# Activations split in one go, dependent sums spread over turns, and an eleventh chunk as seven block products

## The chip, the cores and the metric

The kernel runs on one core of one Trainium2 chip. The metric is the device time of one execution in microseconds. Five engines work side by side, each in the order of its own instruction stream: PE (matrix products; PEld is its weight load), DVE (elementwise, also on sums), ACT (elementwise with a function), POOL, and SP, which here only issues transfers. They wait for each other through semaphores.

## The reference, cut to what matters

One layer of a hybrid decoder trunk on 256 rows of 1024 features, all in float32. The change lies in its last part, the MLP, where D_FF is 4096:

```python
n = RMSNorm(x)
h = x + W_mix_out(g_conv * ConformerConv(n) + g_attn * DSA(n))
h = h + CrossAttn(RMSNorm(h), RMSNorm(mem))
hf = _rmsnorm(h, norm_ffn_g[l]) @ w_ff1[l]
h = h + jnp.square(jax.nn.relu(hf)) @ w_ff2[l]
return _rmsnorm(h, norm_final_g)
```

## The kernel before

**Numbers.** A float32 operand is kept as two parts, a high one (ACT copies it into a rounded type) and a low one (DVE subtracts the high one from the operand). A product is three matmuls, high by high, high by low and low by high (`mm3`, L348). So every weight costs ACT and DVE one pass each before PE can use it.

**The MLP stage.** It is the last stage, from about 325 us on. The 4096 hidden features are cut into 16 chunks of 256. Chunk c has a first weight f1(c), 1024 by 256, cut into two sides of 128 columns, and a second weight f2(c), 256 by 1024. The loop at L1304 takes c from 0 to 12 and works two chunks ahead on the first product. For a chunk in `SEVEN` an iteration has six turns, in this order on PE: `first(c+2, side 0)`, the f2(c) pieces `left` and `last`, `first(c+2, side 1)`, and the pieces `outer` and `inner`. `first` is 24 matmuls of 256 columns; the four pieces are 6, 3, 6 and 6 matmuls of 512 columns. What follows chunk 12 is written out by hand from L1316 on.

**Seven or eight block products.** Hidden chunk times f2(c) is a 2 by 2 block product for each of the two row blocks. A chunk not in `SEVEN` does it as eight block products of 512 columns (24 matmuls). A chunk in `SEVEN` (L60) does it as seven (21 matmuls), in the manner of Strassen: some of the factors are sums of blocks. The sums of f2 are made by DVE (`seven`, L214: `outer` makes two sums in one instruction, `inner` two more, each needing the one before), the differences of the hidden blocks by DVE too (`fn`, L1179). Sums and their split copies live in the pool `t8`.

**Weights.** `load` (L164) issues the next 1 MB weight from HBM on SP's queue into one of three buffers `raw`, so it waits until the weight three places earlier has been read to the end. f1 and f2 alternate in the stream, so f2(c+1) goes into the buffer of f1(c+2). `high_jobs` is a queue of splitting jobs in the order in which PE wants the pieces. Every turn calls `split_ahead` (L314): `split_low` (L280) lets DVE make the low part of the job of the turn before, and then runs the sums of the second job in the queue, if it has any; `split_high` (L273) takes the first job and lets ACT make its high part. The load of a later weight is called from the low part of a weight's last piece (L269, L246).

**Chains.** What follows a first product is a generator (`activation`, L1164), moved on by one step at every `tick` (L318), one tick per turn: ACT applies relu and squares, DVE makes the differences, ACT makes the high part `fs`, DVE the low part. Before, side 0 and side 1 are squared and split each on its own, and for a chunk in `SEVEN` side 1 has three differences in one step. `x.done()` (L1309) runs chains by further ticks until chunk c's are at their end.

**PSUM.** A first product goes to a bank of the tag `mm` (L143), which has two. From chunk 2 on the block product `7` holds one of them to the end of the loop (L1228), so all first products share the other: PE may start `first(c+2, side 1)` only after ACT has read side 0 out of it (the relu at L1166).

Of the kernel before, what the change touches and what calls it, by code (L numbers as in the profile page):

```python
# [8 lines left out]
F32 = mybir.dt.float32  # L9
# [7 lines left out]
P = 128  # L17
# [39 lines left out]
HALVES = 6  # L57
EARLY = (3,)
WHOLE = (("conv", 0),)
SEVEN = (2, 3, 4, 6, 7, 8, 9, 10, 11, 12)  # L60
JOINED = 13
BY_HALVES = tuple(("f1", i) for i in (4, 5, 6, 7))

# [51 lines left out]
def block_kernel(ctx, tc, x, xt, mem, memt, wst, wki, vecs, convw, gout, out):  # L115
# [21 lines left out]
    def w2(name, dt=F32, shape=(P, 512)):  # L137
        return work.tile(list(shape), dt, tag="w2", bufs=8, name=name)

    def bank(tag, bufs, name):  # L140
        return psum.tile([P, 512], F32, tag=tag, bufs=bufs, name=name)

# [58 lines left out]

    class Stage:

        def __init__(self, key, high, before=None, slot=True):
            self.key, self.high, self.before, self.slot = key, high, before, slot
            if not slot:
                elsewhere.add(key)

        def prepare(self):
            if self.before:  # L210
                self.before()
                self.before = None

    def seven(key, c, raw):  # L214

        b = raw.rearrange("p (k h n) -> p k h n", k=2, h=2)
        flat = raw.rearrange("p (j n) -> p j n", j=4)
        sums = []

        def outer():  # L220
            sums.append(t8(f"sums{c}", F32, (P, 4, 512)))
            dve.tensor_tensor(out=sums[0][:, 0:2, :], in0=flat[:, 0:4:3, :],
                              in1=flat[:, 1:2, :].to_broadcast([P, 2, 512]), op=ALU.add)

        def inner():
            t = sums[0]
            dve.tensor_tensor(out=t[:, 2, :], in0=t[:, 1, :], in1=flat[:, 0, :], op=ALU.add)
            dve.tensor_tensor(out=t[:, 3, :], in0=t[:, 2, :], in1=flat[:, 2, :], op=ALU.add)

        def stage(name, src_of, n, before=None):  # L230
            def high():
                src = src_of()
                if before:
                    both = t8(f"{name}{c}", F32R, (P, 2, 2, 512))
                    hi, lo = both[:, 0], both[:, 1]
                else:
                    hi = highs.tile([P, N_CHUNK // 2], F32R, tag="hi", name=f"hi{c}{name}")
                    lo = lows.tile([P, N_CHUNK // 2], F32R, tag="lo", name=f"lo{c}{name}")
                    hi, lo = (w[:, : n * 512].rearrange("p (j n) -> p j n", j=n) for w in (hi, lo))
                act(hi, src, AF.Copy)  # L240
# [9 lines left out]
            return Stage((*key, name), high, before, not before)  # L250

        return [stage("left", lambda: b[:, :, 0, :], 2), stage("last", lambda: flat[:, 3:4, :], 1),
                stage("outer", lambda: sums[0][:, 0:2, :], 2, outer), stage("inner", lambda: sums[0][:, 2:4, :], 2, inner)]

    def high(key, c, raw, ns, q, last):
        n = ns.stop - ns.start
# [16 lines left out]
    def split_high():  # L273
        if high_jobs and (not high_jobs[0].slot or nsplit[0] - nused[0] < HALVES - held[0]):
            job = high_jobs.pop(0)
            nsplit[0] += job.slot
            job.prepare()
            job.high()

    def split_low():  # L280
        if low_jobs:
            low_jobs.pop(0)()
        if len(high_jobs) > 1:
            high_jobs[1].prepare()

    nsplit, nused, held = [0], [0], [1]

# [149 lines left out]
    load()  # L437
    zero = w2("zero")
    nc.vector.memset(zero, 0.0)
    zero_r = cst.tile([P, 512], F32R, name="zero_r")  # L440
    nc.vector.tensor_copy(zero_r, zero)
    ident = cst.tile([P, P], F32, name="ident")
    make_identity(nc, ident)
# [6 lines left out]
    ki2 = cst.tile([P, S], F32, name="ki2")  # L450

    nc.scalar.activation(half, half, AF.Sigmoid, bias=0.0, scale=0.0)
    nc.gpsimd.memset(half, -0.5)
# [185 lines left out]
    tick()  # L639
    wi = cst.tile([P, 2, 8], F32, name="wi")  # L640

    bias = [cst.tile([P, P * (qb + 1)], F32, name=f"bias{qb}") for qb in range(2)]

    def causal(t, qb, value):
        tail = t[:, qb * P :]
# [19 lines left out]
    def index_scores():  # L665
# [3 lines left out]
        dve.tensor_copy(wi, ps[:, :16].rearrange("p (r h) -> p r h", r=2))  # L669
        for qb in range(2):  # L670
            nk = P * (qb + 1)
            score = cst.tile([P, nk], F32, name=f"score{qb}")
# [488 lines left out]
    start(turn_rows())  # L1161
    start(ff_scale())

    def activation(c, ct, ps, t, sh, sl):  # L1164
        if ps.shape[1] == S:
            act(t[:, ct, :], ps, AF.Relu)  # L1166
        else:
            yield from merge(t[:, ct, :], ps)
            yield
            act(t[:, ct, :], t[:, ct, :], AF.Relu)  # L1170
        act(t[:, ct, :], t[:, ct, :], AF.Square)
        yield
        flat = t.rearrange("p k (r n) -> p (k r) n", r=2)
        if c not in SEVEN:
            cs = [(slice(2 * ct, 2 * ct + 2), flat[:, 2 * ct : 2 * ct + 2, :])]
        else:
            cs = [(slice(1, 3), flat[:, 2:4, :]) if ct else (slice(0, 1), flat[:, 0:1, :])]
        if ct and c < JOINED:
            n = w2(f"fn{c}", F32, (P, 4, P))  # L1179
            if c in SEVEN:  # L1180
                dve.tensor_tensor(out=n[:, 0:2, :], in0=flat[:, 1:2, :].to_broadcast([P, 2, P]), in1=flat[:, 0:4:3, :],
                                  op=ALU.subtract)
                dve.tensor_tensor(out=n[:, 2, :], in0=flat[:, 0, :], in1=n[:, 1, :], op=ALU.subtract)
                dve.tensor_tensor(out=n[:, 3, :], in0=flat[:, 2, :], in1=n[:, 2, :], op=ALU.subtract)
                cs.append((slice(3, 7), n))
            else:
                dve.tensor_tensor(out=n[:, 0:2, :], in0=flat[:, 0:4:2, :], in1=flat[:, 1:4:2, :], op=ALU.subtract)
                cs.append((slice(4, 6), n[:, 0:2, :]))
        for js, src in cs:
            act(sh[:, js, :], src, AF.Copy)  # L1190
        yield
        for js, src in cs:
            dve.tensor_tensor(out=sl[:, js, :], in0=src, in1=sh[:, js, :].bitcast(F32), op=ALU.subtract)

    class Hidden:

        def __init__(self, c):
            self.c, self.jobs = c, []
            parts = t8(f"fs{c}", F32R, (P, 2, 7, P))
            self.hi, self.lo = parts[:, 0], parts[:, 1]  # L1200
            self.t = w2(f"ft{c}", F32, (P, 2, S))

        def after(self, ct, ps):
            self.jobs.append(start(activation(self.c, ct % 2, ps, self.t, self.hi, self.lo)))
# [2 lines left out]
            return self.hi[:, j, :], self.lo[:, j, :]  # L1207

        def row(self, k, rb):
            return self.of(2 * k + rb)  # L1210

        def done(self):
            for job in self.jobs:
# [31 lines left out]
            seventh(x, name)  # L1245
            tick()

    TERMS = {"left": (("1", 0), ("2", 1)), "last": (("3", 6),), "outer": (("5", 4), ("7", 3)), "inner": (("6", 5), ("4", 2))}

    def seventh(x, name):  # L1250
        w = weights("f2", x.c, name, None)
# [18 lines left out]
        return ap.rearrange("p (k f) -> p k f", f=P)  # L1270

    def last_residual(rb, ps, lo, hi):
        h = h_rm[:, lo // P : hi // P, rb, :]
        ps = by_tiles(ps)
        dve.scalar_tensor_tensor(out=h, in0=ps, scalar=r2[0][:, rb : rb + 1], in1=h, op0=ALU.mult, op1=ALU.add)

    def last_squares(rb, n, lo, hi):

        h = h_rm[:, lo // P : hi // P, rb, :]
        junk = w2(f"junk_o{rb}{n}")  # L1280
        act(by_tiles(junk[:, : hi - lo]), h, AF.Square, scale=1.0 / 32, accum_out=ss[:, rb, n : n + 1])
        if hi == D:
            dve.scalar_tensor_tensor(out=ss[:, rb, 0:1], in0=ss[:, rb, 0:1], scalar=EPS,
                                     in1=ss[:, rb, 1:2] if n == 2 else zero_c, op0=ALU.add, op1=ALU.add)
        dve.tensor_tensor(out=by_tiles(hg[:, rb, lo:hi]), in0=h, in1=by_tiles(g_out[lo // 512][:, lo % 512 : lo % 512 + hi - lo]), op=ALU.mult)

    def last_norm(rb, n):
        ms = small.tile([P, 1], F32, tag="mso", name=f"ms_o{rb}")
        dve.tensor_tensor(out=ms, in0=ss[:, rb, 0:1], in1=ss[:, rb, n : n + 1], op=ALU.add)
        nc.gpsimd.tensor_tensor(out=rs[:, rb : rb + 1], in0=ms, in1=half[:, 0:1], op=ALU.pow)  # L1290
        scale = rs[:, rb : rb + 1]
        for n, (lo, hi) in enumerate(((0, 352), (352, 704), (704, D))):
            cols = hg[:, rb, lo:hi]
            if n < 2:
                dve.tensor_scalar(cols, cols, scale, None, ALU.mult)
            else:
                act(cols, cols, AF.Copy, scale=scale)
            (nc.scalar if n == 2 else nc.sync).dma_start(out[rb, :, lo:hi], cols)

    def add_to(rb, hf, ps, scales):  # L1300
        h = h_rm[:, 4 * hf : 4 * hf + 4, rb, :]
        dve.scalar_tensor_tensor(out=h, in0=by_tiles(ps), scalar=scales[:, rb : rb + 1], in1=h, op0=ALU.mult, op1=ALU.add)

    for c in range(JOINED):  # L1304
        hidden.append(Hidden(c + 2))
        x, later = hidden[c], hidden[c + 2]
        wide = c not in SEVEN and c != 5
        first(later, 0, wide)
        x.done()  # L1309
        if c in (0, 1, JOINED - 1):  # L1310
            split_ahead()
        half_of(x, 0)
# [130 lines left out]
```

## Time and profile before

| | us |
|---|---|
| runs | 505.32, 505.08, 504.98; median 505.08 |
| profiled execution, its own time | 505.25 |
| its span, first to last instruction | 503.5 |
| mean granted TensorE clock | 0.998 |
| ACT busy over the span | 349.1 |
| DVE busy from 394.76 to 458.55 us (63.79 us) | 62.01 |
| PE busy in the same stretch | 63.66 |

The span is 1.75 us shorter than the execution's time; that difference lies ahead of the first and behind the last instruction. Durations below come from this one execution. An instruction's duration holds a tail in which the next one on the engine may already run, so what an engine spends on a row of instructions is read from their starts. Views used are the page, the chain of work that ended last, the waits, and the timeline, whose rows give start, duration, engine, line, operation, output<-inputs and in brackets the idle time ahead of it. `lo` and `hi` are parts of a weight; `hi70left` belongs to the weight with number 70 in the stream, and f2(c) has number 54+2c.

### The profile page before, as it was taken

How to read it: one execution, taken by the hardware profiler on the slowest of the kernel's cores; microseconds unless marked ns; L12 is line 12 of the kernel's file. 1: busy time of each engine (PE TensorE's matmuls, PEld its weight loads, DVE VectorE, ACT ScalarE, POOL GpSimd, SP SyncE). 2: the span in 40 equal slices, each digit the busy share in tenths (PEclk: the TensorE clock that was granted, in tenths of full speed). 3: DMA queues.
4: the chain of work that ended last, by engine and by line, in shares of the span. 5: the costliest groups of instructions: out<-in, count | busy, mean ns of one | idle time of the engine just before them, and what ended most of it. 6: DMA issues, size and time to landing. Idle time of an engine off the chain costs nothing.

```text
span 503.5 us, 8292 instructions
## 1 busy us (share of the span) xinstructions
PE 493.6 (98%) x3119; PEld 444.1 (88%) x3119; DVE 459.9 (91%) x858; ACT 349.1 (69%) x639; POOL 31.6 (6%) x49
## 2 busy tenths in 40 slices
PE   7999999999999999999999999999999999999995
PEld 5999998888888888888889999988989899988984
DVE  5999999999999799999988986888999899999994
ACT  7657777788656676668756667586777677777832
POOL 2002212221021100000000000000000000000000
PEclk9999999999999999999999999999999999999999
DMA  8949678899787744345645454368855645544602
GB/s 312 381 184 280 185 191 261 226 246 262 225 265 215 191 148 144 119 158 197 246 169 218 175 174 161 127 192 214 239 181 184 235 159 206 221 178 168 251 1 84
DMA packets 27225, 100.36 MB, mean 199 GB/s; under 512 B 10656, under 2 KB 11552, under 8 KB 17200
## 3 DMA queue, kind: packets, MB, share of 16 engines
q1 hardware_dynamic: 23120, 92.90, 53.4%
q0 software_dynamic: 3632, 6.59, 7.3%
q8 instruction: 24, 0.39, 0.3%
q10 hardware_dynamic: 432, 0.33, 0.2%
q14 instruction: 17, 0.14, 0.1%
HBM read 91.16 MB, written 1.05 MB: 183 GB/s over the span
## 4 chain that ended last, share of the span: by engine, by line
PE 62%; DVE 18%; ACT 7%; DMA 7%; issue 5%; POOLq 0%; POOL 0%; DVEq 0%; ACTq 0%
PE ps_conv L80 10%; DMA raw<-in_wst_dram 6%; PE ps_f L80 6%; DVE lo L80 5%; PE ps_ao L80 4%; PE ps_q L80 4%; PE ps_k L80 4%; PE ps_ga L80 4%; PE ps_gc L80 4%; PE ps_v L80 4%; PE ps_xo L80 3%; DVE sums L80 3%; PE ps_qi L80 2%; PE ps_xk L80 2%; PE ps_p L80 2%
## 5 line engine op out<-in xcount | busy, mean ns | idle before, releaser
L80 DVE TENSOR_TENSOR lo<-raw,hi 128x1024 fp32r<-128x1024 f32 x141 | 170.5, 1214 | 5.2 <-ACT hi L263 5.1
L263 ACT ACTIVATE hi<-raw 128x1024 fp32r<-128x1024 f32 x141 | 146.7, 1046 | 2.0 <-DMA raw<-in_wst_dram 2.0
L80 PE MATMUL ps_f<-ff_p,hi 128*128 128x256 f32 (+1 forms) x448 | 92.8, 299 | 0.6 <-ACT ft L1166 0.3
L80 DVE SCALAR_TENSOR_TENSOR acc<-u,cw,acc 128x234 f32<-128x234 f32 (+29 forms) x190 | 78.0, 461 | 0.3
L80 PEld LDWEIGHTS ps_f<-ff_p,hi 128*128 128x128 f32 x448 | 72.8, 191 | 5.8 <-ACT ft L1166 2.0
L80 PE MATMUL ps_f<-ff_p,lo 128*128 128x256 f32 x256 | 70.9, 282 | 0.0
L80 PEld LDWEIGHTS ps_f<-ff_p,lo 128*128 128x128 f32 x256 | 48.8, 191 | 0.6
L80 PE MATMUL ps_conv<-n_p,hi 128*128 128x256 f32 x224 | 41.0, 285 | 0.0
L80 PEld LDWEIGHTS ps_conv<-n_p,hi 128*128 128x128 f32 x224 | 34.9, 192 | 0.8 <-issue 0.7
L80 PE MATMUL ps_conv<-n_p,lo 128*128 128x256 f32 x112 | 31.7, 283 | 0.0
L588 POOL DMA_DIRECT2D acc<-products x25 | 21.6, 864 | 125.1 <-ACT products L587 50.1
L80 PE MATMUL ps_p<-hi,fs 128*128 128x512 f32 (+1 forms) x88 | 27.2, 372 | 0.0
L80 PE MATMUL ps_q<-n_p,hi 128*128 128x512 f32 x64 | 23.6, 406 | 0.0
L80 PE MATMUL ps_k<-n_p,hi 128*128 128x512 f32 x64 | 23.5, 407 | 0.0
L80 PE MATMUL ps_ao<-o_p,hi 128*128 128x512 f32 x64 | 22.6, 401 | 0.0
L80 PE MATMUL ps_co<-u_p,hi 128*128 128x512 f32 (+1 forms) x80 | 22.2, 351 | 0.0
L80 PE MATMUL ps_mix<-mix_p,hi 128*128 128x512 f32 (+1 forms) x80 | 22.2, 351 | 0.0
L80 PE MATMUL ps_ga<-n_p,hi 128*128 128x512 f32 x64 | 22.0, 396 | 0.0
L80 PE MATMUL ps_gc<-n_p,hi 128*128 128x512 f32 x64 | 22.0, 396 | 0.0
L587 ACT ACTIVATE products<-u,cw 128x231 f32<-128x231 f32 (+24 forms) x50 | 21.9, 489 | 0.0
L80 PEld LDWEIGHTS ps_conv<-n_p,lo 128*128 128x128 f32 x112 | 21.5, 192 | 0.0
L80 PE MATMUL ps_v<-hi,n_p 128*128 128x512 f32 x64 | 19.9, 389 | 0.0
(386 smaller groups left out, 1215.8 us busy)
## 6 DMA issues: line engine op xcount, KB each, us to landing
raw<-in_wst_dram SPq DMA_DIRECT2D x76, 1024.0 KB, 4.9
acc<-products POOLq DMA_DIRECT2D x25, 256.0 KB, 5.3
raw<-in_wst_dram SPq DMA_DIRECT2D x12, 512.0 KB, 7.6
x_rm<-in_x_dram SPq DMA_DIRECT2D x2, 512.0 KB, 4.2
mem_rm<-in_mem_dram SPq DMA_DIRECT2D x1, 1024.0 KB, 8.9
mem_t<-in_memt_dram SPq DMA_DIRECT2D x1, 1024.0 KB, 10.9
h_t<-in_xt_dram SPq DMA_DIRECT2D x1, 1024.0 KB, 7.0
h_rm<-turned SPq DMA_DIRECT2D x16, 64.0 KB, 5.6
```

Of the source, the lines that this page charges most:

```text
L80: return fn(*args, **kwargs)
L263: act(hi, raw[:, ns], AF.Copy)
L587: act(prod[:, a, s:], u[:, t, : S - s], AF.Copy, scale=cw[:, t, TAPS - 1 - s : TAPS - s])
L588: nc.gpsimd.dma_start(acc[:, ts, :], prod, accum_op=ALU.add)
```

## The change

Three things change in the MLP stage; tiles are also packed differently.

- `SEVEN` gets chunk 5, so chunks 2 to 12 are all done as seven block products.
- The sums of f2 become steps. `split_low` runs one step of the first of the next three jobs that has any, and not all sums of the second job at once. `inner` is two steps.
- The activation waits for both sides: side 0 only gets its relu, then both are squared in one instruction, the differences are made in three separate steps, and high and low parts are one instruction each over seven blocks (six or four for the other chunks). The last chunk, 15, keeps a split by sides. Row blocks are taken in swapped order so that the seven blocks lie side by side; `h_rm` and the output rows are indexed to match.
- `x.done()` goes ahead of `first(later, 0, wide)`.
- `ft` has a pool tag of its own with two buffers; `zero_r`, `ki2`, `bias` and `score` share that space before the MLP.

```diff
-SEVEN = (2, 3, 4, 6, 7, 8, 9, 10, 11, 12)
+SEVEN = (2, 3, 4, 5, 6, 7, 8, 9, 10, 11, 12)
...
+    def w4(name, dt=F32, shape=(P, KT, P)):
+        return work.tile(list(shape), dt, tag="w4", bufs=2, name=name)
...
-        def inner():
+        def inner(j):
             t = sums[0]
-            dve.tensor_tensor(out=t[:, 2, :], in0=t[:, 1, :], in1=flat[:, 0, :], op=ALU.add)
-            dve.tensor_tensor(out=t[:, 3, :], in0=t[:, 2, :], in1=flat[:, 2, :], op=ALU.add)
+            dve.tensor_tensor(out=t[:, j, :], in0=t[:, j - 1, :], in1=flat[:, 2 * j - 4, :], op=ALU.add)
...
-                stage("outer", lambda: sums[0][:, 0:2, :], 2, outer), stage("inner", lambda: sums[0][:, 2:4, :], 2, inner)]
+                stage("outer", lambda: sums[0][:, 0:2, :], 2, (outer,)),
+                stage("inner", lambda: sums[0][:, 2:4, :], 2, (lambda: inner(2), lambda: inner(3)))]
...
             nsplit[0] += job.slot
-            job.prepare()
+            while job.steps:
+                job.step()
             job.high()
 
     def split_low():
         if low_jobs:
             low_jobs.pop(0)()
-        if len(high_jobs) > 1:
-            high_jobs[1].prepare()
+        for job in high_jobs[:3]:
+            if job.steps:
+                job.step()
+                break
...
+    def part(c, t, js, sh, sl):
+        act(sh[:, js, :], t, AF.Copy)
+        yield
+        dve.tensor_tensor(out=sl[:, js, :], in0=t, in1=sh[:, js, :].bitcast(F32), op=ALU.subtract)
...
     def activation(c, ct, ps, t, sh, sl):
...
+        yield from relu(ps, t[:, 2 * ct : 2 * ct + 2, :].rearrange("p r n -> p (r n)"))
+        if ct == 0:
+            return
+        act(t[:, 0:4, :], t[:, 0:4, :], AF.Square)
+        yield
+        js = slice(0, 4)
+        if c in SEVEN:
+
+            dve.tensor_tensor(out=t[:, 4:6, :], in0=t[:, 0:1, :].to_broadcast([P, 2, P]), in1=t[:, 1:3, :], op=ALU.subtract)
             yield
+            dve.tensor_tensor(out=t[:, 6, :], in0=t[:, 1, :], in1=t[:, 5, :], op=ALU.subtract)
+            yield
+            dve.tensor_tensor(out=t[:, 7, :], in0=t[:, 3, :], in1=t[:, 6, :], op=ALU.subtract)
+            yield
+            js = slice(1, 8)
...
+        yield from part(c, t[:, js, :], slice(0, js.stop - js.start), sh, sl)
...
         wide = c not in SEVEN and c != 5
+        x.done()
         first(later, 0, wide)
-        x.done()
```

More of the change, by code (lines that the diff above doesn't have):

```diff
@@ L202, in block_kernel, with __init__, step @@
     class Stage:
-        def __init__(self, key, high, before=None, slot=True):
-            self.key, self.high, self.before, self.slot = key, high, before, slot
+        def __init__(self, key, high, steps=(), slot=True):
+            self.key, self.high, self.steps, self.slot = key, high, list(steps), slot
             if not slot:
                 elsewhere.add(key)
[L209 to L212, printed above, removed]
+        def step(self):
+            self.steps.pop(0)()
     def seven(key, c, raw):
@@ L223, in outer, with stage @@
                               in1=flat[:, 1:2, :].to_broadcast([P, 2, 512]), op=ALU.add)
-        def inner():
+        def inner(j):
             t = sums[0]
-            dve.tensor_tensor(out=t[:, 2, :], in0=t[:, 1, :], in1=flat[:, 0, :], op=ALU.add)
-            dve.tensor_tensor(out=t[:, 3, :], in0=t[:, 2, :], in1=flat[:, 2, :], op=ALU.add)
-        def stage(name, src_of, n, before=None):
+            dve.tensor_tensor(out=t[:, j, :], in0=t[:, j - 1, :], in1=flat[:, 2 * j - 4, :], op=ALU.add)
+        def stage(name, src_of, n, steps=()):
             def high():
                 src = src_of()
-                if before:
+                if steps:
                     both = t8(f"{name}{c}", F32R, (P, 2, 2, 512))
@@ L248, in high @@
                 low_jobs.append(low)
-            return Stage((*key, name), high, before, not before)
+            return Stage((*key, name), high, steps, not steps)
         return [stage("left", lambda: b[:, :, 0, :], 2), stage("last", lambda: flat[:, 3:4, :], 1),
-                stage("outer", lambda: sums[0][:, 0:2, :], 2, outer), stage("inner", lambda: sums[0][:, 2:4, :], 2, inner)]
+                stage("outer", lambda: sums[0][:, 0:2, :], 2, (outer,)),
+                stage("inner", lambda: sums[0][:, 2:4, :], 2, (lambda: inner(2), lambda: inner(3)))]
     def high(key, c, raw, ns, q, last):
@@ L439, in block_kernel @@
     nc.vector.memset(zero, 0.0)
-    zero_r = cst.tile([P, 512], F32R, name="zero_r")
+    zero_r = w4("zero_r", F32R, (P, 512))
     nc.vector.tensor_copy(zero_r, zero)
@@ L449, in block_kernel @@
     nc.gpsimd.memset(table, 0.0)
-    ki2 = cst.tile([P, S], F32, name="ki2")
+    picked = w4("picked", F32, (P, D))
+    ki2 = picked[:, 3 * S :]
     nc.scalar.activation(half, half, AF.Sigmoid, bias=0.0, scale=0.0)
@@ L640, in block_kernel @@
     wi = cst.tile([P, 2, 8], F32, name="wi")
-    bias = [cst.tile([P, P * (qb + 1)], F32, name=f"bias{qb}") for qb in range(2)]
+    bias = [picked[:, :P], picked[:, P : 3 * P]]
     def causal(t, qb, value):
@@ L671, in index_scores @@
             nk = P * (qb + 1)
-            score = cst.tile([P, nk], F32, name=f"score{qb}")
+            score = picked[:, (3 + qb) * P : (3 + qb) * P + nk]
             per = 512 // nk
@@ L1162, in block_kernel @@
     start(ff_scale())
-    def activation(c, ct, ps, t, sh, sl):
[L1165 to L1168, printed above, removed]
-            yield
[L1170 to L1193, printed above, removed]
@@ new lines, in relu, with by_halves @@
+    def relu(ps, t):
+        if ps.shape[1] == S:
+            act(t, ps, AF.Relu)
+        else:
+            yield from merge(t, ps)
+            yield
+            act(t, t, AF.Relu)
+    def part(c, t, js, sh, sl):
+        act(sh[:, js, :], t, AF.Copy)
+        yield
+        dve.tensor_tensor(out=sl[:, js, :], in0=t, in1=sh[:, js, :].bitcast(F32), op=ALU.subtract)
+    def by_halves(c, ct, ps, t, sh, sl):
+        js = slice(2 * ct, 2 * ct + 2)
+        yield from relu(ps, t[:, js, :].rearrange("p r n -> p (r n)"))
+        act(t[:, js, :], t[:, js, :], AF.Square)
+        yield
+        yield from part(c, t[:, js, :], js, sh, sl)
@@ new lines, in activation @@
+    def activation(c, ct, ps, t, sh, sl):
+        if c == 15:
+            yield from by_halves(c, ct, ps, t, sh, sl)
+            return
+        yield from relu(ps, t[:, 2 * ct : 2 * ct + 2, :].rearrange("p r n -> p (r n)"))
+        if ct == 0:
+            return
+        act(t[:, 0:4, :], t[:, 0:4, :], AF.Square)
[3 more added lines that the diff above has]
+            dve.tensor_tensor(out=t[:, 4:6, :], in0=t[:, 0:1, :].to_broadcast([P, 2, P]), in1=t[:, 1:3, :], op=ALU.subtract)
+            yield
+            dve.tensor_tensor(out=t[:, 6, :], in0=t[:, 1, :], in1=t[:, 5, :], op=ALU.subtract)
+            yield
+            dve.tensor_tensor(out=t[:, 7, :], in0=t[:, 3, :], in1=t[:, 6, :], op=ALU.subtract)
+            yield
+            js = slice(1, 8)
+        elif c < JOINED:
+            dve.tensor_tensor(out=t[:, 4:6, :], in0=t[:, 1:4:2, :], in1=t[:, 0:4:2, :], op=ALU.subtract)
+            yield
+            js = slice(0, 6)
+        yield from part(c, t[:, js, :], slice(0, js.stop - js.start), sh, sl)
@@ L1200, in __init__ @@
             self.hi, self.lo = parts[:, 0], parts[:, 1]
-            self.t = w2(f"ft{c}", F32, (P, 2, S))
+            self.t = w4(f"ft{c}")
         def after(self, ct, ps):
@@ L1209, in row @@
         def row(self, k, rb):
-            return self.of(2 * k + rb)
+            return self.of(2 * k + 1 - rb)
         def done(self):
@@ L1246, in half_of @@
             tick()
-    TERMS = {"left": (("1", 0), ("2", 1)), "last": (("3", 6),), "outer": (("5", 4), ("7", 3)), "inner": (("6", 5), ("4", 2))}
+    TERMS = {"left": (("1", 0), ("2", 2)), "last": (("3", 6),), "outer": (("5", 4), ("7", 3)), "inner": (("6", 5), ("4", 1))}
     def seventh(x, name):
@@ L1272, in last_residual @@
     def last_residual(rb, ps, lo, hi):
-        h = h_rm[:, lo // P : hi // P, rb, :]
+        h = h_rm[:, lo // P : hi // P, 1 - rb, :]
         ps = by_tiles(ps)
-        dve.scalar_tensor_tensor(out=h, in0=ps, scalar=r2[0][:, rb : rb + 1], in1=h, op0=ALU.mult, op1=ALU.add)
+        dve.scalar_tensor_tensor(out=h, in0=ps, scalar=r2[0][:, 1 - rb : 2 - rb], in1=h, op0=ALU.mult, op1=ALU.add)
     def last_squares(rb, n, lo, hi):
-        h = h_rm[:, lo // P : hi // P, rb, :]
+        h = h_rm[:, lo // P : hi // P, 1 - rb, :]
         junk = w2(f"junk_o{rb}{n}")
@@ L1297, in last_norm @@
                 act(cols, cols, AF.Copy, scale=scale)
-            (nc.scalar if n == 2 else nc.sync).dma_start(out[rb, :, lo:hi], cols)
+            (nc.scalar if n == 2 else nc.sync).dma_start(out[1 - rb, :, lo:hi], cols)
     def add_to(rb, hf, ps, scales):
-        h = h_rm[:, 4 * hf : 4 * hf + 4, rb, :]
-        dve.scalar_tensor_tensor(out=h, in0=by_tiles(ps), scalar=scales[:, rb : rb + 1], in1=h, op0=ALU.mult, op1=ALU.add)
+        h = h_rm[:, 4 * hf : 4 * hf + 4, 1 - rb, :]
+        dve.scalar_tensor_tensor(out=h, in0=by_tiles(ps), scalar=scales[:, 1 - rb : 2 - rb], in1=h, op0=ALU.mult, op1=ALU.add)
     for c in range(JOINED):
```

## The prediction

> **What bounds the kernel now.** I read the page first, then the waits of PE's weight loads, the chain of work that ended last, and the timeline of one iteration. The page:
>
> ```profile
> span 503.5 us, 8292 instructions
> PE 493.6 (98%) x3119; PEld 444.1 (88%) x3119; DVE 459.9 (91%) x858; ACT 349.1 (69%) x639; POOL 31.6 (6%) x49
> PE 62%; DVE 18%; ACT 7%; DMA 7%; issue 5%; POOLq 0%; POOL 0%; DVEq 0%; ACTq 0%
> ```
>
> PE is busy 98% of the span, yet only 62% of the chain is PE: much of the rest lies in the MLP, where two engines run nearly full. The waits of PE's weight loads from 300 us on name one cause:
>
> ```profile
> PEld ps_f L80 <- ACT ft L1166: 2.0, 4, 0.7
> ```
>
> Four times a first product waited for ACT's relu, the read that frees the only bank of `ps_f`. On PE itself the stalls are these, from the timeline (chunk 3, then chunk 11):
>
> ```profile
> 371.88 0.39 PE L80 MATMUL ps_p<-hi60last,fs 128*128 128x512 f32 x1
> 372.14 0.36 ACT L1166 ACTIVATE ft<-ps_f 128x256 f32<-128x256 f32 x1
> 372.56 0.39 PE L80 MATMUL ps_f<-ff_p,hi 128*128 128x256 f32 x1 [0.29 <-ACT ft L1166]
> ...
> 458.03 0.39 PE L80 MATMUL ps_p<-hi76last,fs 128*128 128x512 f32 x1
> 458.55 0.30 PEld L80 LDWEIGHTS ps_f<-ff_p,hi 128*128 128x128 f32 x2 [0.56 <-ACT ft L1166]
> ```
>
> Now the chain, whose rows are start, duration and what:
>
> ```profile
> 346.18 5.38 DMA raw<-in_wst_dram
> ...
> 352.67 1.23 DVE lo58left L80
> ...
> 357.37 6.24 DMA raw<-in_wst_dram
> ...
> 368.60 1.22 DVE lo L80
> ...
> 388.51 4.84 DMA raw<-in_wst_dram
> ...
> 394.76 3.14 PE ps_f L80 x24
> 397.90 2.75 PE ps_p L80 x12
> 400.64 2.87 PE ps_f L80 x24
> 403.52 2.07 PE ps_p L80 x9
> 405.58 2.89 PE ps_f L80 x24
> ...
> 410.59 1.21 DVE lo L80
> 411.82 4.81 DMA raw<-in_wst_dram
> 416.65 1.07 ACT hi70left L240
> ...
> 421.62 1.23 DVE lo L80
> ```
>
> Two things are to be seen. **PE's own need** for an iteration with seven products is 397.90 to 405.58 plus 2.89, so 10.57 us. From the 2.07 us of nine 512-column matmuls (from 403.52) one costs 0.229, so the matmul at 371.88 has to be followed by a first product at 372.11, and the stall there is 0.45; at 458.03 it is 0.29, and a third, which I count like that one, ends at 394.76, behind a 4.84 us transfer. The first product after a stall takes 3.14 and not 2.87 to 2.89, of which I count 0.1 as restart. All three make 1.3 us.
>
> **The loop beside PE**: the low part of a piece of f1 ends (410.59 plus 1.21), its buffer is free, f2's transfer goes (411.82), lands after 4.81, ACT makes `hi70left`, and DVE goes on to the next such low part at 421.62. One turn of this loop is 11.04 us, 0.47 more than PE needs. PE lives on a reserve that shrinks by that much per iteration, and stalls when it is used up; chunk 5, with eight products and no sums, gives reserve back. The DVE side of one turn, from the timeline:
>
> ```profile
> 406.71 1.22 DVE L80 TENSOR_TENSOR lo68left<-raw,hi68left 128x1024 fp32r<-128x1024 f32 x1
> 407.85 0.69 DVE L80 TENSOR_TENSOR lo68last<-raw,hi68last 128x512 fp32r<-128x512 f32 x1
> 408.45 1.22 DVE L80 TENSOR_TENSOR sums<-raw 128x1024 f32<-128x1024 f32 x1
> 409.59 0.42 DVE L80 TENSOR_TENSOR fn<-ft 128x256 f32<-128x256 f32 x1
> 410.04 0.62 DVE L80 TENSOR_TENSOR fn<-ft,fn 128x128 f32<-128x128 f32 x2
> 410.58 1.22 DVE L80 TENSOR_TENSOR lo<-raw,hi 128x1024 fp32r<-128x1024 f32 x1
> 411.71 1.41 DVE L80 TENSOR_TENSOR sums<-sums,raw 128x512 f32<-128x512 f32 x2
> 413.04 0.42 DVE L80 TENSOR_TENSOR fs<-ft,fs 128x256 fp32r<-128x256 f32 x1
> 413.37 0.69 DVE L80 TENSOR_TENSOR fs<-fn,fs 128x512 fp32r<-128x512 f32 x1
> 413.98 1.22 DVE L80 TENSOR_TENSOR outer<-sums,outer 128x1024 fp32r<-128x1024 f32 x1
> 415.11 1.22 DVE L80 TENSOR_TENSOR inner<-sums,inner 128x1024 fp32r<-128x1024 f32 x1
> 416.25 1.22 DVE L80 TENSOR_TENSOR lo<-raw,hi 128x1024 fp32r<-128x1024 f32 x1
> 417.38 0.28 DVE L80 TENSOR_TENSOR fs<-ft,fs 128x128 fp32r<-128x128 f32 x1
> 417.75 1.23 DVE L80 TENSOR_TENSOR lo70left<-raw,hi70left 128x1024 fp32r<-128x1024 f32 x1
> ```
>
> DVE has no gap over 0.1 us in it: 11.04 us from `lo68left` to `lo70left`. So two bounds meet here, DVE's own work and the loop through the transfer.
>
> **The change, part by part.** By starts, 1024 elements cost DVE 1.14, 512 cost 0.60.
>
> *DVE's work.* The differences (409.59 to 410.58, 0.99) lose their waits on each other once each has a turn of its own: 0.34 for 256 (413.04 to 413.37), and 0.21 for each of 128 (the second of the pair ends the 0.99). That is 0.76, 0.23 less. The two sums cost 1.33 together (411.71 to 413.04) and 0.61 each apart, 0.11 less. The three `fs` cost 0.33, 0.61 and up to 0.37; one of 896, between 0.60 for 512 and 1.14 for 1024, is 1.00 by their slope, 0.31 less. Sum: 11.04 less 0.65, 10.39 us. That alone is below PE's 10.57.
>
> *The loop.* What counts is where the pieces go. In the turn of `last`, the queue holds last, f1 side 1, outer: the new `split_low` makes the low part of `left` and then the sum for outer. In the next turn it makes the low part of `last` and then the first of the two inner sums; the tick behind adds the first difference, 256 wide. Only then comes the low part of f1 that frees the buffer. So the loop is: low part to transfer 1.24 (410.58 to 411.82), transfer and wake-up 4.83 (to 416.65), ACT 1.10 (to 417.75), `left` 1.14, outer sum 1.14, `last` 0.60, inner sum 0.61, difference 0.34: **11.00 us**. The 0.99 of differences leaves the loop, but an inner sum and a difference, 0.95, come in. DVE's saved 0.6 becomes a wait for the transfer ahead of each `left`. Two iterations on the transfer's leg is a little shorter:
>
> ```profile
> 433.92 1.66 SPq L176 DMA_DIRECT2D raw<-in_wst_dram  x2
> ...
> 438.67 1.06 ACT L240 ACTIVATE hi74left<-raw 128x1024 fp32r<-128x1024 f32 x1 [0.48 <-DMA raw<-in_wst_dram]
> ```
>
> From issue to ACT's start it is 4.75 and not 4.83, which makes the loop 10.92. I take the middle, 10.96.
>
> *The relu.* The second inner sum now follows the freeing low part at once, so ACT's `inner` copy and the relu behind it come 0.72 earlier (411.71 to 413.04 becomes 0.61), once, not per iteration.
>
> *ACT and the tiles.* One square and one copy of a pair go, all beside DVE and the transfer: in the loop ACT has one `hi`, 1.10, and waits for the rest, so its gain is worth nothing, and if that cover were gone 0.3 to 0.4 per turn (the 0.36 of an `ft` row is the nearest). The shared tile of `bias`, `score` and `ki2` moves no work; I take 0 for it, up to 0.5 us once if a wait appears.
>
> *Chunk 5.* PE loses three matmuls, 0.69 us. DVE and ACT get a full loop turn, and the place where the reserve came back is gone. Eleven turns of the loop follow on each other.
>
> *`x.done()` ahead.* At chunk 0 it now runs three ticks ahead of the weights' split: they hold the sums of squares, differences, and one 768-wide split. I estimate that the low part which frees the first buffer comes some 4 us later, of which the transfers behind it hide most; the row at 352.67 I place 0.9 later, bounds 0 and 1.6. The matmuls for the row scale also move ahead of `first(2, 0)` and can hold PE some 0.4; while the loop is the limit that costs nothing, else 0.4.
>
> *The start.* From `lo58left` (352.67) to the next freeing low part it was 3.46 (the transfer's start, 357.37, less 1.24); it becomes 1.14 + 1.14 + 0.60 + 0.61 and a 256-wide merge, 0.34, so 3.83, 0.4 more. The 6.24 us transfer at 357.37 ran among small ones (`h_rm`), which the ticks now issue earlier: between 0 and 1.42 comes back, I take 0.7. The next leg was 3.89 (368.60 less 357.37, 6.24 and 1.10); with the `fs` of chunk 3, which is a tick late because its first products are wide, it becomes 1.14 + 1.14 + 0.60 + 0.61 + 1.00 + 0.34 = 4.83, 0.9 more. With the relu's 0.72: 0.9 + 0.4 - 0.7 + 0.9 - 0.7 = 0.8 later at the first product of 372.56; bounds -0.45 (PE is not ready before 372.11) and 2.2.
>
> *The sum.* From 372.56 to 458.55 the old kernel took 85.99 for eight iterations. Eight turns of 10.96 are 87.7: 1.7 more, the three stalls and the 0.69 of chunk 5 included, for PE now waits in each of them. With 0.8 it is 2.5 us. Behind 458.55 the two kernels do the same; ACT and DVE have less in it, perhaps 0.2. The forecast is 2.3 us more: 505.8 in span for 503.5, 507.6 for this execution's 505.25, **507.4 against the median of 505.08**. The bounds of this case: 8 x 10.92 with -0.45 gives 505.8, 8 x 11.00 with 2.2 gives 509.1.
>
> **Two rules of the Trainium skill.** The row first: 1 MB took 4.81 here. The page DMA: Bandwidth & Descriptors (section Anatomy of one DMA) gives 2.0 us fixed plus the bytes at 436 GB/s; by that a 1 MiB transfer is an estimated 4.4, the loop 10.6, and the first rival below would come true. The trace disagrees by 0.4, and the measurement decides. Second: the next load of f1 is issued 0.7 earlier in the changed kernel, close behind f2's. The same page (Queues, rings and completion order) says that each DMA engine takes descriptors in ring order; by that the second load can't delay the first, and 4.8 stays. The trace agrees as far as it goes: 4.81, with another load issued right behind; the 6.24 among small transfers speaks the other way.
>
> **The rivals.**
>
> *First, PE becomes the bound (faster).* If the loop is below 10.57, no stall is left. Then the 1.3 of stalls and the 0.69 go, and the 0.4 at chunk 0 comes: 1.6 less, 503.5. For it: DVE's work is 10.39, and its near lack of gaps is what the old trace shows. Against it: the transfer's leg, which the change doesn't shorten. It decides from 0.4 us less per turn, for instance if the first inner sum fell behind the freeing low part (11.00 - 0.61 = 10.39).
>
> *Second, the two cancel.* If the start is not later (-0.45) and the loop's mean is 10.8, the sum is 8 x 10.8 - 85.99 - 0.45 = 0.0: 505.1.
>
> *Third, f2's transfer suffers from the load close behind.* With a third of the 1.42 between 6.24 and 4.82, each turn has 0.47 more, eight of them 3.8: 511.2.
>
> *The change doesn't do what it says:* the steps may sit in other turns, if the queue is a job longer or shorter than I derived; that ends in the first rival's time, and is in its chance.
>
> **How the numbers follow.** Forecast 0.55, first rival 0.27, second 0.13, third 0.05. What can be told from no change here is about 0.2%, 1.0 us. The forecast's case lies above 506.1 but for a twentieth, so slower is 0.57, same 0.16, faster 0.27. The range has to reach the first rival, 503.5, with half a microsecond for its terms, and the forecast's case up to 508.8, which leaves out its last part and the third rival: 503.0 to 508.8. The forecast's own range is 505.8 to 509.1.
>
> **What would show it.** Right: in chunks 4 to 11 DVE waits some 0.5 us ahead of every `left` part for ACT's copy, that one for the transfer; starts of `left` lie 10.9 to 11.0 apart; PE waits for the relu ahead of `first(c+2, side 1)` in most of these iterations, 0.4 each; DVE's share falls. Wrong: `left` 10.57 apart, ACT's relu waiting for PE, no wait of a weight load for the relu. The derivation stands on the order of the turns; if the sums lie elsewhere on DVE, the loop's sum is void.

## The result, and the profile after

The changed kernel takes **510.35 us** (median of five runs, 509.21 to 510.80) where the old one takes 505.08. The ratio is 1.0097, with an interval of 1.008 to 1.0115: slower by about 1%. Forecast were 507.4 in a range of 503.0 to 508.8, so the direction was right and the size was not. The profiled execution took 510.8 us, the longest of the five; its span is 509.0.

The page of the changed kernel, with the span, the busy time of each engine, the shares of the chain that ended last, and one of the costliest groups:

```profile
span 509.0 us, 8232 instructions
PE 495.9 (97%) x3116; PEld 443.8 (87%) x3116; DVE 460.2 (90%) x837; ACT 344.5 (68%) x598; POOL 31.7 (6%) x49
PE 56%; DVE 18%; DMA 12%; ACT 8%; issue 5%; POOLq 0%; POOL 0%; DVEq 0%; ACTq 0%; SPq 0%
L80 PEld LDWEIGHTS ps_f<-ff_p,hi 128*128 128x128 f32 x448 | 72.3, 191 | 11.8 <-ACT ft L1171 8.5
```

DMA's share of the chain went from 7% to 12%, PE's from 62% to 56%. ACT has 41 instructions less and 4.6 us less work, as the change intends, and the kernel is slower all the same. The waits of PE's weight loads from 300 us on say where it shows (what waits, on what: us in total, times, longest):

```profile
PEld ps_f L80 <- ACT ft L1171: 8.5, 11, 1.8
PEld ps_ff L80 <- DVE sums_ff L80: 0.7, 1, 0.7
```

Eleven waits for the relu where there were four, 8.5 us where there were 2.0, and one new wait for the row scale. One turn of the loop, from DVE's timeline (start, duration, what, and in brackets the idle time ahead):

```profile
413.04 1.23 DVE L80 TENSOR_TENSOR lo68left<-raw,hi68left 128x1024 fp32r<-128x1024 f32 x1 [0.64 <-ACT hi68left L240]
414.19 1.22 DVE L80 TENSOR_TENSOR sums<-raw 128x1024 f32<-128x1024 f32 x1
415.32 0.69 DVE L80 TENSOR_TENSOR lo68last<-raw,hi68last 128x512 fp32r<-128x512 f32 x1
415.93 0.68 DVE L80 TENSOR_TENSOR sums<-sums,raw 128x512 f32<-128x512 f32 x1
416.53 0.42 DVE L80 TENSOR_TENSOR ft<-ft 128x256 f32<-128x256 f32 x1
416.86 1.22 DVE L80 TENSOR_TENSOR lo<-raw,hi 128x1024 fp32r<-128x1024 f32 x1
418.00 0.68 DVE L80 TENSOR_TENSOR sums<-sums,raw 128x512 f32<-128x512 f32 x1
418.60 0.28 DVE L80 TENSOR_TENSOR ft<-ft 128x128 f32<-128x128 f32 x1
418.80 1.22 DVE L80 TENSOR_TENSOR outer<-sums,outer 128x1024 fp32r<-128x1024 f32 x1
419.94 0.28 DVE L80 TENSOR_TENSOR ft<-ft 128x128 f32<-128x128 f32 x1
420.14 1.22 DVE L80 TENSOR_TENSOR inner<-sums,inner 128x1024 fp32r<-128x1024 f32 x1
421.27 1.22 DVE L80 TENSOR_TENSOR lo<-raw,hi 128x1024 fp32r<-128x1024 f32 x1
422.41 1.09 DVE L80 TENSOR_TENSOR fs<-ft,fs 128x896 fp32r<-128x896 f32 x1
423.98 1.23 DVE L80 TENSOR_TENSOR lo70left<-raw,hi70left 128x1024 fp32r<-128x1024 f32 x1 [0.48 <-ACT hi70left L240]
```

The turn is 10.94 us long (413.04 to 423.98). DVE is busy for 10.46 of it; the other 0.48 is the wait for `hi70left`, whose weight has just landed. The first inner sum (415.93) and the first difference (416.53) stand ahead of the low part at 416.86, the one that frees the buffer. So DVE was relieved and the loop was not.

PE's first products after the stalls that open and close the eight turns (PE's timeline):

```profile
376.05 0.51 PE L80 MATMUL ps_f<-ff_p,hi 128*128 128x256 f32 x2 [1.21 <-ACT ft L1171]
...
463.77 0.50 PE L80 MATMUL ps_f<-ff_p,hi 128*128 128x256 f32 x2
```

These are the rows that stood at 372.56 and 458.55 before. Between them lie 87.72 us for 85.99. The span grew by 5.5: **3.5 before the eight turns, 1.7 in them, 0.3 behind them.** Now the chain at the start of the loop:

```profile
338.57 5.52 DMA raw<-in_wst_dram
...
348.36 5.40 DMA raw<-in_wst_dram
353.78 1.07 ACT hi58left L240
354.87 1.23 DVE lo58left L80
356.10 1.14 DVE sums L80
357.43 0.60 DVE lo58last L80
358.04 0.60 DVE sums L80
358.64 1.00 DVE fs L80
359.97 1.14 DVE lo L80
361.17 5.71 DMA raw<-in_wst_dram
...
372.90 1.14 DVE lo L80
```

Taken row by row against the chain of the old kernel, with what was forecast:

| step | before | after | change | forecast |
|---|---|---|---|---|
| start of `lo58left` | 352.67 | 354.87 | +2.20 | +0.9 |
| from there to the transfer of f2(3), less 1.24 | 3.46 | 5.06 | +1.60 | +0.4 |
| that transfer | 6.24 | 5.71 | -0.53 | -0.7 |
| from its end, less 1.10, to the next freeing low part | 3.89 | 4.92 | +1.03 | +0.9 |
| from there to the first product | 3.96 | 3.15 | -0.81 | -0.7 |
| sum | | | +3.49 | +0.8 |

Two rows are wrong, the first two. The second can be read off the chain: beside the five terms of the forecast there is a 1.00 us `fs` at 358.64, and between 356.10 plus 1.14 and 357.43 a difference of 0.20. The first belongs to `x.done()`: the transfer at 338.57 is f2(1)'s, which started at 334.46 in the old kernel. ACT's copies at its landing, old kernel first:

```profile
340.25 1.06 ACT L263 ACTIVATE hi<-raw 128x1024 fp32r<-128x1024 f32 x1 [0.59 <-DMA raw<-in_wst_dram]
344.12 1.06 ACT L264 ACTIVATE hi<-raw 128x1024 fp32r<-128x1024 f32 x1 [4.30 <-DMA raw<-in_wst_dram]
```

From there to the start of f2(2)'s transfer it was 5.93 us (to 346.18) and is 4.24 (to 348.36): in the old kernel `fs` and `fn` of the activation stand between on ACT and DVE, and in the changed one they are over by then. So the 4.1 us at f2(1) shrink to 2.2.

### The profile page after: what moved, and what is told of

It reads as the page before. It is cut to its first block, busy times and chain, and to the rows that moved or that the text cites. A ratio compares the mean times of both kernels' runs of the same rounds, so it can differ in the third digit from the quotient of the medians.

```text
span 509.0 us, 8232 instructions
## 1 busy us (share of the span) xinstructions
PE 495.9 (97%) x3116; PEld 443.8 (87%) x3116; DVE 460.2 (90%) x837; ACT 344.5 (68%) x598; POOL 31.7 (6%) x49
## 4 chain that ended last, share of the span: by engine, by line
PE 56%; DVE 18%; DMA 12%; ACT 8%; issue 5%; POOLq 0%; POOL 0%; DVEq 0%; ACTq 0%; SPq 0%
DMA raw<-in_wst_dram 12%; PE ps_conv L80 9%; DVE lo L80 5%; PE ps_ao L80 4%; PE ps_q L80 4%; PE ps_k L80 4%; PE ps_ga L80 4%; PE ps_gc L80 4%; DVE sums L80 4%; PE ps_v L80 4%; PE ps_xo L80 3%; ACT hi L264 3%; PE ps_qi L80 2%; PE ps_xk L80 2%; PE ps_xv L80 2%
## 5 line engine op out<-in xcount | busy, mean ns | idle before, releaser
L80 DVE TENSOR_TENSOR lo<-raw,hi 128x1024 fp32r<-128x1024 f32 x139 | 168.3, 1216 | 6.3 <-ACT hi L264 6.0
L264 ACT ACTIVATE hi<-raw 128x1024 fp32r<-128x1024 f32 x139 | 144.7, 1046 | 5.3 <-DMA raw<-in_wst_dram 5.3
L240 ACT ACTIVATE inner<-sums 128x1024 fp32r<-128x1024 f32 x11 | 11.7, 1062 | 22.7 <-DVE sums L80 22.7
L80 PE MATMUL ps_p<-hi,fs 128*128 128x512 f32 (+1 forms) x72 | 21.7, 367 | 0.0
```

Of the source, the lines that this page charges most:

```text
L80: return fn(*args, **kwargs)
L264: act(hi, raw[:, ns], AF.Copy)
```

## The experiments

The theory to be tested had three parts. The loop beside PE sets the pace, and what counts is which DVE instructions stand inside it. The place of `x.done()` at chunk 0 delays the start of that loop. Chunk 5 was the place where reserve came back. The main rival was that DVE's total work, or some cost of the new activation, sets the pace. The old kernel ran beside each group of experiments, with medians of 505.13 (1 to 4), 505.78 (5 to 8) and 505.37 (9 to 11). The ratios are to these runs; a difference in microseconds between groups can be off by some 0.7.

**1. `x.done()` later at chunk 0** (`e1_done_late`).

```diff
     tile_b(ps, w, f2, wide=wide)
+    if before:
+        before.done()
     x.after(side, ps if wide else ps[:, :S])
...
-        x.done()
-        first(later, 0, wide)
+        if c:
+            x.done()
+        first(later, 0, wide, x)
```

> Only the place of x.done() at chunk 0 goes back: behind the matmuls of first(2, 0) and its split, ahead of its activation. Theory A (the start's delay of 3.5 us at the first product of 376.05 is 2.2 of this, 1.6 of the longer leg behind lo58left, 0.9 of the leg behind lo60left, less 0.5 and 0.7): lo58left back near 352.7 instead of 354.9, the wait of PE at the row-scale matmuls gone, the whole 2.2 us less, 508.1 (507.4 to 508.7); the turns of the loop behind it stay 10.9 to 11.0. Rival B (the start is set by the new activation alone): 510.0 to 510.6.

Measured: 508.2 us (median of four, 508.13 to 510.13), ratio to the old kernel 1.0069 (1.0051 to 1.0087), so 2.15 less than the changed kernel by the medians. The means differ by 1.5, for one of the four runs took 510.13, and the two intervals overlap a little; the size is therefore rough. The profile is of that slowest run (f2(3)'s transfer took 6.33 us in it):

```profile
353.20 1.23 DVE L80 TENSOR_TENSOR lo58left<-raw,hi58left 128x1024 fp32r<-128x1024 f32 x1 [1.38 <-ACT hi58left L240]
```

1.67 of the 2.20 are gone. This is more than the 0.9 that the forecast gave to the step, and just more than its upper bound of 1.6.

**2. Chunk 5 as eight block products again** (`e2_no5`): `SEVEN` without 5, all else as changed.

> Chunk 5 is done as eight block products again, all else as in the changed kernel. Theory A (each turn of the loop costs 0.4 more than PE needs, and chunk 5 gave reserve back): the stalls of chunks 5 to 9 go, those of 3 and 4 stay, 0.69 of matmuls comes back; 508.5 (507.6 to 509.2). Rival B (chunk 5 costs nothing, the loss is all in the start): 510.3 plus 0.7, 511.0.

Measured: 509.4 (508.29 to 510.58), ratio 1.0084 (1.0066 to 1.0102). That is 0.95 less than with chunk 5 as seven in the medians, less than was expected, and the two intervals overlap, so the times alone don't settle it; the profiled run, 508.29, is the fastest of the four. Its PE timeline at chunk 5, where the eight products end:

```profile
396.42 0.39 PE L80 MATMUL ps_p<-hi,fs 128*128 128x512 f32 x1
397.82 0.38 PE L80 MATMUL ps_f<-ff_p,hi 128*128 128x256 f32 x1 [1.00 <-ACT ft L1171]
```

PE stalls there and no more in the chunks 6 to 11: chunk 5 does give reserve back, but part of it is lost at once in this stall. That it is the late start which is paid for here is my reading and not shown. From `first(5, side 1)` to the end of the span this execution needs 132.25 us (374.25 to 506.5), the changed kernel 132.95.

**3. The sums as before** (`e3_old_sums`). Activation, chunk 5 and `x.done()` stay as changed.

```diff
-        for job in high_jobs[:3]:
-            if job.steps:
-                job.step()
-                break
+        for job in high_jobs[1:2]:
+            while job.steps:
+                job.step()
```

> The sums are made as before the change, all of the second job in the queue at once, so outer's behind the low part of last and both inner sums behind the low part that frees the buffer; activation, chunk 5 and x.done() stay. DVE gets 0.11 us more work per turn. Theory A (the loop through the transfer binds, and the first inner sum is what fills it up): the loop is 10.39, DVE 10.5, both under PE's 10.57, so the stalls of chunks 4 to 11 go: 506.6 (506.0 to 507.6). Rival B (DVE's total work binds, or the number of its instructions): not faster, 510.3 to 511.2.

Measured: 505.95 (median of ten, 505.0 to 507.65), ratio 1.0012 (1.0002 to 1.0021), a little below the range expected. The spread of the sums alone costs 4.4 us, the largest part of the change. DVE has no less to do than in the changed kernel, so DVE's total was not what bound it. The profile is of its slowest run, with f2(3)'s transfer at 6.34 us; its `first(5, side 1)` starts at 376.07, as late as in the changed kernel, but only one more stall follows (0.28 us, behind the matmul at 397.06). From there on its turns are 10.49 us:

```profile
411.37 1.22 DVE L80 TENSOR_TENSOR lo68left<-raw,hi68left 128x1024 fp32r<-128x1024 f32 x1
...
421.86 1.22 DVE L80 TENSOR_TENSOR lo70left<-raw,hi70left 128x1024 fp32r<-128x1024 f32 x1
```

**4. Both undone** (`e4_old_sums_late`: the edits of 1 and 3).

> Both of the edits of the first and the third run. Theory A: the gains add, 504.4 (503.8 to 505.4), PE without a stall from chunk 4 on. Rival B: 510.

Measured: 505.29 (504.19 to 506.37, ten runs), ratio 1.0002 (0.999 to 1.0013): as fast as the old kernel, with the new activation and chunk 5 as seven still in it. The runs fall into two groups, five from 504.2 to 504.9 and five from 505.7 to 506.4. The profiled run is one of the lower group (504.2). Its only wait of a first or block product from 300 us on is this one, at chunk 0:

```profile
PEld ps_p L80 <- DVE fs L80: 1.2, 1, 1.2
```

and one of its turns reads, on DVE:

```profile
407.63 1.22 DVE L80 TENSOR_TENSOR lo68left<-raw,hi68left 128x1024 fp32r<-128x1024 f32 x1
408.77 0.69 DVE L80 TENSOR_TENSOR lo68last<-raw,hi68last 128x512 fp32r<-128x512 f32 x1
409.37 1.22 DVE L80 TENSOR_TENSOR sums<-raw 128x1024 f32<-128x1024 f32 x1
410.51 0.42 DVE L80 TENSOR_TENSOR ft<-ft 128x256 f32<-128x256 f32 x1
410.84 1.22 DVE L80 TENSOR_TENSOR lo<-raw,hi 128x1024 fp32r<-128x1024 f32 x1
411.98 1.41 DVE L80 TENSOR_TENSOR sums<-sums,raw 128x512 f32<-128x512 f32 x2
...
418.12 1.22 DVE L80 TENSOR_TENSOR lo70left<-raw,hi70left 128x1024 fp32r<-128x1024 f32 x1
```

Both inner sums now stand behind the low part at 410.84. The stretch from `left` to that low part is 3.21 us and no longer 3.82 (413.04 to 416.86), no wait for ACT is left, and a turn is 10.49. That is below PE's 10.57, and PE stalls no more in eleven chunks: the first rival of the prediction, which came about when the sum left the loop, as the prediction had said it would.

**5 and 6. The same work inside the loop and outside it.** In the changed kernel one low part of 512 elements is written twice per turn in the chunks 4 to 11. In `e5_extra_in` it is that of `last`, ahead of the freeing low part; in `e6_extra_out` it is half of `inner`, behind it.

```diff
         dve.tensor_tensor(out=lo, in0=src, in1=hi.bitcast(F32), op=ALU.subtract)
+        if name == "last" and 4 <= key[1] <= 11:
+            one = slice(0, 1)
+            dve.tensor_tensor(out=lo[:, one, :], in0=src[:, one, :], in1=hi[:, one, :].bitcast(F32), op=ALU.subtract)
```

> The changed kernel with one instruction more per turn on DVE for chunks 4 to 11: the low part of the piece last is written twice (128x512, 0.60 us by starts), between the landing of the transfer and the low part that frees the next buffer. Theory A (the loop through the transfer binds): each turn is 0.60 longer, eight of them 4.8, 515.1 (514.3 to 516). Rival B (DVE has 0.5 us idle per turn, so small work hides): 510.3 to 511.2.

> The changed kernel with an instruction of the same size per turn at another place: half of the low part of the piece inner is written twice (128x512, 0.60), while DVE's loop waits for the transfer. Theory A: DVE idles some 0.5 us ahead of each left part, which takes the most of it: 0 to 0.1 per turn, 510.3 to 511.3. Rival B (DVE's total work binds): as much as the run with the instruction inside the loop, 514 to 515.

Measured: 515.78 with the work inside (ratio 1.0213, 1.019 to 1.0236), 511.17 with the same work outside (1.0115, 1.0093 to 1.0137). The turn at 402 of each, `e5_extra_in` first:

```profile
402.00 1.23 DVE L80 TENSOR_TENSOR lo66left<-raw,hi66left 128x1024 fp32r<-128x1024 f32 x1 [0.52 <-ACT hi66left L240]
...
404.28 1.41 DVE L80 TENSOR_TENSOR lo66last<-raw,hi66last 128x512 fp32r<-128x512 f32 x2
...
413.68 1.23 DVE L80 TENSOR_TENSOR lo68left<-raw,hi68left 128x1024 fp32r<-128x1024 f32 x1 [0.50 <-ACT hi68left L240]
```

```profile
402.07 1.22 DVE L80 TENSOR_TENSOR lo66left<-raw,hi66left 128x1024 fp32r<-128x1024 f32 x1
...
409.16 1.95 DVE L80 TENSOR_TENSOR inner<-sums,inner 128x1024 fp32r<-128x1024 f32 x2
...
413.17 1.22 DVE L80 TENSOR_TENSOR lo68left<-raw,hi68left 128x1024 fp32r<-128x1024 f32 x1
```

Inside, a turn is 11.68 and DVE still waits 0.5 ahead of `left`: the loop grew by the whole instruction. Outside, the turn is 11.10, 0.1 more than the mean of 10.98, and the wait of 0.5 has been filled: DVE has no gap left there, and its own work is now the bound. One and the same instruction costs 0.7 or 0.1 us per turn by its place.

**7. The old kernel with chunk 5 as seven** (`e7_before_5`): `SEVEN` with 5, nothing else.

> The kernel before with chunk 5 in SEVEN and nothing else of the change. Theory A: turns of 11.0 from chunk 3 to 11 without the relief of chunk 5: 372.56 plus 88.0 against 458.55, 2.0 us more: 507.1 (506.4 to 508.2). Rival B (chunk 5 alone is worth its three matmuls): 504.4.

Measured: 507.36 (507.27 to 507.80), ratio 1.0035 (1.0021 to 1.0049). PE has 0.69 us less to do, and the kernel takes 1.6 us more than the old one beside it (505.78; 1.8 by the ratio). From the first product after the stall of chunk 3 to that of chunk 11 its profile has 88.50 us (372.18 to 460.68) for 85.99. The waits of its weight loads from 300 us on, in place of the four of before:

```profile
PEld ps_f L80 <- ACT ft L1166: 5.7, 9, 0.9
```

The eight products of chunk 5 were worth more as a pause for the loop than they cost on PE.

**8. A better version?** `e8_rows2` is the kernel of 4 with the small transfers of `h_rm` issued two per tick, so that they are over before f2(3)'s transfer. It was to remove the upper group of runs.

```diff
         for b in range(4):
-            yield
+            if b % 2 == 0:
+                yield
```

> The fourth run's kernel (sums as before, x.done() late at chunk 0), with the small transfers of h_rm issued two per tick instead of one, so that they are through before f2(3) is loaded. Theory A' (the runs of that kernel fall in two groups, 504.2 to 504.9 and 505.7 to 506.4, because the transfer of f2(3) takes 4.8 or 6.3 us among the small ones): one group, 504.0 to 504.8. Rival B (the groups come from elsewhere, or the earlier small transfers delay f2(1) as much): 504.2 to 506.4 as before.

Measured: 504.66 (median of twelve, 504.25 to 506.80), ratio 0.9989 (0.9976 to 1.0002). Eight runs lie from 504.2 to 505.0, four from 505.8 to 506.8: the groups are still there, without a small transfer near f2(3)'s, so these are not what makes them. Its median is 1.1 us below the old kernel's beside it, but the interval of the ratio just reaches 1, so a gain is not shown.

**9. `x.done()` between the two places** (`e9_mid`): the kernel of 4, with `before.done()` between `split_ahead()` and `tile_b` of `first(2, side 0)`.

> The kernel of e4 (chunk 5 as seven, activation in one go, sums as before, x.done() late at chunk 0) with x.done() of chunk 0 ahead of the matmuls of first(2, side 0), yet behind its split. What it should take away is the stall of 0.9 us at 337.4 in e4, where PE waits for the low part of hidden chunk 0; what it brings back is a wait of the row-scale matmuls, 0.58 in the changed kernel. Theory (the weights' split stays early, so the loads and the start of the loop stay as in e4, and PE's reserve is spent in no later stall): 0.3 us less than e4, 504.0 to 504.6 in the lower group of runs, 505.5 to 506.2 in the upper. Rival (PE still waits for the same chain, only in another place): the same as e4, 504.2 to 504.9 and 505.7 to 506.4.

Measured: 505.04 (504.75 to 506.32, eleven runs), ratio 0.9998 (0.9989 to 1.0007). The theory did not come true: nine of the runs lie from 504.75 to 505.48, above the range that it gave, and the ratio is that of kernel 4 (1.0002) within the noise, as the rival had it. The stall was swapped for a longer one, which I had taken at 0.58 from the changed kernel.

```profile
PEld ps_ff L80 <- DVE sums_ff L80: 1.6, 1, 1.6
```

Behind the weights' split, the sums for the row scale come later on DVE, and the weight load waits for them 1.6 us here, 0.7 in the changed kernel.

**10 and 11. The kernel of 4 twice more, for its profile.**

> The kernel of e4 once more, for its profile. Its runs fell into two groups, 504.2 to 504.9 and 505.7 to 506.4. Theory: the upper group is a slower transfer of f2(3), the one that opens the loop: above 505.5 it takes 6 us or more and PE waits for the relu ahead of first(5, side 1); below 505 it takes 4.7 to 5.0 and no stall follows. Rival: the groups differ elsewhere, and f2(3) takes 4.7 to 5.0 in both.

> As e10, a further look at the same kernel, so that both groups have a profile: f2(3) in 6 us or more with a stall behind it where the time is above 505.5, in 4.7 to 5.0 and without one where it is below 505; by the rival 4.7 to 5.0 in both.

Measured: 510.1 and 504.37, one run each. In both, f2(3)'s transfer takes 4.8 to 4.9 us, and behind it a weight load waits 0.2 us and PE does not stall. So a slower f2(3) was not what the execution of 510.1 lost its time to. It lost it ahead of the MLP, where DVE adds up the convolution; the waits of PE's weight loads and DVE's timeline of `e10_again`:

```profile
PEld ps_s L80 <- DVE k L80: 4.4, 1, 4.4
```

```profile
190.73 0.48 DVE L80 SCALAR_TENSOR_TENSOR acc<-u,cw,acc 128x246 f32<-128x246 f32 x1 [5.26 <-DMA acc<-products]
```

The last accumulating transfer on POOL's queue came late, DVE stood before it for 5.26 us, and PE behind DVE. It was late because it was issued late, at 184.01 and not at 169.58 as in `e11_again`: these transfers took 6.7 us to land in the median, 5.2 in the other execution, and POOL waited for the earlier ones 56.8 us in all, 34.0 in the other. Why they were slower is not shown. From the first `ps_f` matmul to the end of the span this execution needs 179.7 us (328.63 to 508.3), the other 179.6 (322.97 to 502.6), the old kernel 180.7 (322.82 to 503.5). Whether the upper group near 506 comes from the same place is **open**: no profile shows one of its runs.

## Why the prediction was wrong in size, step by step

**The loop: right.** That the change relieves DVE but not the loop was the heart of the forecast, with 10.96 us per turn and 87.7 for eight. Measured are 10.98 on average (`left` starts at 379.87 and, seven turns on, at 456.71) and 87.72. The order of the pieces on DVE is the derived one, and the wait of 0.5 ahead of each `left` is there in all eight. Experiments 5 and 6 show that the loop sets the pace of the changed kernel, and not DVE's total; 3 and 4 show that the place of the inner sum is what keeps it at 11.

**DVE's own work: right.** 10.39 was worked out. The 10.46 of the turn above counts the tail of `fs`, 0.09, as work, so by starts it is 10.37; in the kernel of 4, where the two inner sums follow each other again, it is 10.49.

**Chunk 5: right.** The reserve that came back there is gone; experiment 7 has it by itself, at 1.6 us against the old kernel beside it, and the eight turns contain it.

**The start: wrong, and this is the step that failed.** The prediction put it at 0.8 with bounds -0.45 and 2.2; it is 3.5 in this execution. Two of its terms were mis-sized. The first is **`x.done()` ahead**, placed at 0.9 with bounds 0 and 1.6. The estimate that the first buffer comes free some 4 us later was good (338.57 for 334.46, 4.1), and the statement that the transfers behind hide most of it was not: 2.2 reached `lo58left`, and experiment 1 took 1.67 of it back. In the other profiles with `x.done()` in this place, experiments 2, 3, 5 and 6, `lo58left` starts at 354.01 to 354.73, 1.3 to 2.1 late, beyond the upper bound in all but one. The bounds were set by judgement and not by following the next two transfers through their buffers. The second is **the leg from `lo58left` to the freeing low part**, placed at 3.83 and measured at 5.06. The `fs` of a chunk with wide first products comes a tick late; the prediction applied this to chunk 3 and its leg, where 4.83 was near the measured 4.92, and forgot that chunk 2 has wide first products as well. Its `fs`, 1.00, and the last difference, 0.20, stand in that leg: 1.2 us, the whole error of the term. It is the firmer of the two: from `lo58left` to f2(3)'s transfer it is 6.30 us in the changed kernel and in experiments 1, 2, 5 and 6, and 4.70 in the old kernel and in experiment 7.

**The relu 0.72 earlier, once: right** (0.81). **The transfer at 357.37: right in sign, by luck.** 0.53 came back for 0.7. But in experiments 2, 5 and 6, whose programs are the changed kernel's up to there, the same transfer took 4.77, 4.73 and 5.83 us, so that it moves more from one execution to the next than the forecast has it move, and that the small transfers slow it is not shown. It moves the start too: the first product that stands at 376.05 stands at 374.25 and 374.56 in experiments 2 and 5, so up to 1.8 of the 3.5 can be this execution's own.

**The row scale: right.** PE waits for the sums at chunk 0 as foreseen, 0.7 on the weight load and 0.41 on PE itself for some 0.4, and since the loop is late anyway it does not show in the eight turns.

**The tail: wrong by half a microsecond.** 0.2 less was forecast, 0.3 more came, and the eleventh of the waits for the relu lies there, behind `outer` of chunk 12. With the 2.7 of the start this is the 3.2 us by which the span missed the forecast.

**The rivals.** The first (PE becomes the bound) did not happen in the change, but did in experiment 4 by the very move that the prediction named, the inner sum behind the freeing low part. The second (the two cancel) asked for a start that is not later and fell with it. The third (f2's transfer suffers from the load close behind) did not come about: from chunk 4 on those transfers land 4.7 to 4.9 us after their issue, with f1's load 0.6 us behind them. The rule of the Trainium skill, page DMA: Bandwidth & Descriptors, section Queues, rings and completion order, that each DMA engine takes descriptors in ring order, agrees with that. The other rule, of its section Anatomy of one DMA, is stated there for transfers that GpSimd (POOL) issues, and these go on SP's queue; the estimate of 4.4 us that the prediction made from it stays below every one of them.

What is shown: the place of the sums costs 4.4 us and the place of `x.done()` 2.15 in the medians (1.5 in the means), each undone alone; both undone give 5.1, less than the sum of the medians, and bring the time of the old kernel back with the new activation and chunk 5 as seven in place. So neither of these two costs time once the inner sum is out of the loop. With the sums as before, `x.done()` costs only 0.66 in the medians (505.95 and 505.29), of runs that scatter by 2 us. Why it is less there is not shown.

## What to carry to other kernels

Where a loop through a transfer runs beside an engine's own work and both are equally long, count the loop's legs by instruction: work taken off the engine was worth nothing here, as it did not leave the leg between the data's arrival and the instruction that frees the buffer, and work moved into that leg was paid in full in every turn. Before all instances of a costlier form are replaced by the cheaper one, look at what its slack feeds: the one chunk with 0.69 us more on PE was the loop's pause. And when a step is moved ahead at the start of a pipeline, follow the transfers that it delays through their buffers up to the first steady turn, for a start that is late is not made up by a loop that has no reserve.

## What the runs showed of the hardware

- The 1 MB transfer of f2(3), which starts at 357 to 361 us in all kernels but one execution, took from 4.73 to 6.34 us in these profiles: 6.24 in the old kernel, 5.71 in the changed one, 6.34 in `e3_old_sums`, 4.86 in `e4_old_sums_late`. Most of its successors in the loop take 4.7 to 5.0. In `e2_no5` and `e5_extra_in`, with the same small transfers ahead of it as in the changed kernel, it took 4.77 and 4.73; in `e8_rows2`, where none is near it, 4.84. So the small transfers don't explain the spread, and the cause is open.
- The accumulating transfers on POOL's queue took 6.7 us to land in the median in one execution and 5.2 in another of the same program; the last of them then held up DVE for 5.26 us and the whole core with it (510.1 for 504.37).
- Two sums of which the second needs the first took 1.33 us in a row and 0.60 each when something else stood between them (413.31 less 411.98 in the kernel of 4; the changed turn above).
